# Operands of the MLP's first product 64 bytes further in memory, in tiles of 2176 bytes, beside a halved scratch for software DMA

## The chip, the cores and the metric

The kernel runs on one core of a Trainium2 chip. The metric is the device time of one execution in microseconds: 784.97 is the median of three runs of the kernel before (784.47 to 785.39). A difference of about 0.2% (1.57 us) is what a measurement of this kernel can tell from none.

## The reference

One layer of an encoder trunk over 512 rows of 1024 numbers: three token-mixing branches with gates, cross-attention into 256 memory tokens, and a squared-ReLU MLP, each sub-layer between two RMS norms. The change touches the last one:

```python
hf = rmsnorm(x, g_norm[l, 4])
yf = jnp.square(jax.nn.relu(hf @ w_up[l])) @ w_down[l]      # 1024 -> 4096 -> 1024
x = x + rmsnorm(yf, g_norm[l, 5])
```

## The kernel before

All products are float32 results made of three fast products. Every operand is split into a high part (a cast on ScalarE, line 152) and a low part (source minus high, on VectorE, line 153), and `mm3` (line 159) adds high by high, high by low and low by high in PSUM. So a weight block of 128 columns and an activation of 256 or 512 columns cost three matmuls, and each matmul has a weight load of its own (engine PEld in the profile, which runs beside PE). All of them are recorded at line 107, so groups of the profile are told apart by tile names.

Memory inside the core (224 KiB in each of 128 partitions, all tiles named by their bytes in one partition) is cut into pools. The pool of **slots** (line 79) has 27 tiles of 512 float32 numbers, 2048 bytes each. Nearly everything of that size passes through it: the parts of the first input `xg`, queries, merged branches `mg`, the residual `x`, scratch, and `xf`, the 8 pairs (high, low) of the normed input of the MLP (line 911), x by channel, channels in the partitions and the 512 rows along the tile. `by_channel` (line 725) writes `xf`. Weights and their parts stand in tiles of 4096 bytes in other pools (`parts_of`, line 117), whose names are `whi`/`wlo`, with a `u` behind for the MLP's first product and a `b` for its second.

The MLP works on quarters of its matrices, with seven block products instead of eight. In the first product (`two`, line 1109) one call makes two blocks of 128 of the 4096 inner channels: seven products of 12 matmuls each, 256 columns of x a time. Numbered as in the code, products 1, 5, 2 and 4 read `xf` (5 reads the second half of `xf0` to `xf3`, which a difference has been written over), products 6, 3 and 7 read the sums `xs6`, `xs3`, `xs7`. These three are made once (`quarters`, line 1040), in tiles of 4096 bytes that the code pushes 64 bytes on by an unused tile of 64 bytes ahead of them (`shift`, lines 1056 to 1066). Products 7 and 4 are held back into the middle of the second product's work. `steps` (line 1304) writes out the order by hand: 13 calls of `two` (steps "V") among 28 products of the second kind (`product`, line 1227, 512 columns of weights a time, activations as the stationary operand), one block made plainly ("U"), and the end (`down`, line 1252). Ahead of them stand five blocks made plainly over each half of the rows (216 matmuls into `ps` and 24 into `t`, 256 columns each, all reading `xf`). Loads and splits for a step are prepared two steps ahead of it.

Matmuls and transposes keep the program's order on TensorE; the other engines take theirs from a scheduler.

DMAs are issued by SyncE in hardware, and by GpSimd in software: 12 loads that add into a gate weight tile, 28 that add into an MLP weight tile, 8 loads of the memory tokens, 2 rows and 8 pieces of x (line 806). The program lets 8 software DMAs be under way: a ninth waits for the first. What GpSimd's DMAs are described by stands in a scratch at the start of the memory, 16384 bytes of each partition where nothing else is asked for.

Places in the built program (bytes in a partition): the weight parts start 64 past a multiple of 128 (832 past a multiple of 2048 all of them), the slots, and so `xf`, do the same, and so do the parts `mh` and `ml` of the memory tokens, which have the tile shape of `xs`. The `xs` tiles start at a multiple of 128 (896 past a multiple of 2048).

Of the kernel before, what the change touches and what calls it, by code (L numbers as in the profile page):

```python
# [10 lines left out]
F32 = mybir.dt.float32  # L11
F32R = mybir.dt.float32r
# [4 lines left out]
P = 128  # L17
D = 1024
S = 512
NT = S // P  # L20
KD = D // P
# [4 lines left out]
NSLOT, NHALF, NBIG = 27, 9, 8  # L26
# [33 lines left out]
def trunk(ctx: ExitStack, tc: tile.TileContext, wkvq, xT, xt0, memT, wst, cst, vec, rows, wsp, wpl, out):  # L60
    nc = tc.nc
# [6 lines left out]
    sl = ctx.enter_context(tc.tile_pool(name="sl", bufs=1))  # L68
# [7 lines left out]
    ones = tn.tile([P, 1], F32, name="ones")  # L76
    mhalf = tn.tile([P, 4], F32, name="mhalf")

    def slot(name, dt=F32, shape=None):
        return sl.tile(shape or [P, S], dt, name=name, tag="slot", bufs=NSLOT)  # L80

    late, extra = [], []

# [3 lines left out]
    def tiny(name, bufs=3):  # L87
        return tn.tile([P, 4], F32, name=name, tag=name, bufs=bufs)

    def pair(name, shape=None):  # L90
        return slot(name + "h", F32R, shape), slot(name + "l", F32R, shape)

    def pair_of(pool, name):
        return tuple(pool.tile([P, S], F32R, name=name + z, tag="act", bufs=2 * KD) for z in "hl")
# [39 lines left out]
    def wtile(i, fence=()):  # L134
        raw, hi, lo = wtiles(i)
        wdma[i] = nc.sync.dma_start(raw, wst[i]).ins
        with ExitStack() as c:
            for ins in fence:
                c.enter_context(tc.issue_after(ins))
            split(hi, lo, raw)  # L140
        return hi, lo
# [36 lines left out]
    def sqacc(sacc, src, first, n, eng=None, order=free):  # L178

        if first:  # L180
            order(nc.scalar.activation(sacc, src, AF.Square))
        else:
            sq = half("sq") if n == HALF else slot("sq")
            order(nc.scalar.activation(sq, src, AF.Square))
            order((eng or nc.vector).tensor_tensor(sacc, sacc, sq, op=ALU.add))

    class Rstd:
# [19 lines left out]
        def copied(self):  # L207
            n = self.t * P
            t = half("rb") if n == HALF else slot("rb")
            self.end = nc.vector.tensor_copy(t, self.spread()).ins  # L210
            return t


    with ExitStack() as c1:
        a = c1.enter_context(tc.tile_pool(name="a", bufs=1))
# [17 lines left out]

        x0 = [slot(f"x0_{k}") for k in range(KD)]
        xg = [pair(f"xg{k}") for k in range(KD)]
        sink = tn.tile([P, 8], F32, name="sink")

# [13 lines left out]
        for k in range(KD):  # L251
            split_scaled(*xg[k], x0[k], vc[:, V_G + k:V_G + k + 1], keep)
            for lo, hi in pieces if not k else [(0, NKVQ * P)]:
                r, h, l = (z[:, lo:hi] for z in raw[k])
# [32 lines left out]
        for b in range(4):  # L287
            q.append(pair(f"q{b}"))
            qend = split(*q[b], scaled(pq[b], f"qs{b}"))
# [342 lines left out]
        def merged(hf):  # L632

            if not mg:
                mg.extend(pair(f"mg{k}") for k in range(KD))
            for k in range(0, KD, 2):
                pt = bank()
                for kk2 in range(2):
                    for tb in range(2):
                        turn(pt[:, kk2 * HALF + tb * P:kk2 * HALF + (tb + 1) * P],  # L640
                             acc[2 * hf + tb, k // 4][:, (k % 4 + kk2) * P:(k % 4 + kk2 + 1) * P])
                for kk2 in range(2):
                    nc.scalar.copy(cut(mg[k + kk2], *halfcut(hf))[0], pt[:, kk2 * HALF:(kk2 + 1) * HALF])
                for kk2 in range(2):
                    hi, lo = cut(mg[k + kk2], *halfcut(hf))
                    end = nc.vector.tensor_tensor(lo, pt[:, kk2 * HALF:(kk2 + 1) * HALF], hi.bitcast(F32),
                                                  op=ALU.subtract).ins
            return end
# [93 lines left out]
    with ExitStack() as c2:  # L742
# [25 lines left out]
        def grow(name, at):  # L768
            g = big(name, F32, [P, 1024])
            nc.gpsimd.dma_start(g, rows[0:1, at:at + 1024].broadcast_to([P, 1024]))  # L770
            return g
# [136 lines left out]


        g3 = grow("g3", 3080)  # L910
        xf = [pair(f"xf{k}") for k in range(KD)]
        wom.update({i: wtile(T_OM + i, oend[0]) for i in (1, 3)})

        pso = {}
# [31 lines left out]
    with ExitStack() as c3:  # L946
        f = c3.enter_context(tc.tile_pool(name="f", bufs=1))
# [493 lines left out]
```

## Time and profile before

| | us |
|---|---|
| median of three runs | 784.97 |
| the profiled execution, whole time | 784.68 |
| its span, first to last instruction | 782.8 |
| PE busy | 773.3 |
| PEld busy | 671.0 |
| VectorE (DVE) busy | 611.5 |
| ScalarE (ACT) busy | 473.4 |
| GpSimd (POOL) busy | 66.6 |

How to read it: busy time is in us and as a share of the span. A matmul's duration holds its way through the array, so matmuls overlap in the records; how fast they follow each other is read from their starts in the timeline. A group's name is output<-moving operand,stationary operand, with the numbers of buffers left out where they end a name; PEld rows carry the name of the matmul that they load for. Granted clock is that of TensorE, 1.00 from the start to 772 us.

### The profile page before, as it was taken

How to read it: one execution, taken by the hardware profiler on the slowest of the kernel's cores; microseconds unless marked ns; L12 is line 12 of the kernel's file. 1: busy time of each engine (PE TensorE's matmuls, PEld its weight loads, DVE VectorE, ACT ScalarE, POOL GpSimd, SP SyncE). 2: the span in 40 equal slices, each digit the busy share in tenths (PEclk: the TensorE clock that was granted, in tenths of full speed). 3: DMA queues.
4: the chain of work that ended last, by engine and by line, in shares of the span. 5: the costliest groups of instructions: out<-in, count | busy, mean ns of one | idle time of the engine just before them, and what ended most of it. 6: DMA issues, size and time to landing. Idle time of an engine off the chain costs nothing.

```text
span 782.8 us, 11476 instructions
## 1 busy us (share of the span) xinstructions
PE 773.3 (99%) x4286; PEld 671.0 (86%) x4286; DVE 611.5 (78%) x931; ACT 473.4 (60%) x884; POOL 66.6 (9%) x93
## 2 busy tenths in 40 slices
PE   9999999999999999999999999999999999999996
PEld 8888878878888888788988899999988998899885
DVE  6488976898658657467759769899888998899866
ACT  7238779666562462444847585876666665567622
POOL 0000000201001000351100020001000100010001
PEclk9999999999999999999999999999999999999998
DMA  8325222745757132564331471776747764766612
GB/s 288 108 82 188 81 82 65 203 105 174 186 187 149 62 116 100 208 207 150 108 108 55 175 208 49 193 188 140 166 147 182 169 143 148 195 146 147 208 52 95
DMA packets 34423, 112.79 MB, mean 144 GB/s; under 512 B 4160, under 2 KB 4288, under 8 KB 34368
## 3 DMA queue, kind: packets, MB, share of 16 engines
q1 hardware_dynamic: 27152, 86.64, 32.8%
q0 software_dynamic: 7072, 25.17, 16.8%
q8 instruction: 33, 0.54, 0.3%
q10 hardware_dynamic: 144, 0.26, 0.1%
q14 instruction: 22, 0.18, 0.1%
HBM read 107.86 MB, written 4.19 MB: 143 GB/s over the span
## 4 chain that ended last, share of the span: by engine, by line
PE 90%; DVE 4%; ACT 4%; issue 1%; POOLq 0%; DVEq 0%; ACTq 0%
PE ps L107 51%; PE y L107 13%; PE v L107 10%; PE t L107 9%; PE z L107 6%; PE ps L110 2%; ACT s L335 2%; ACT s L345 1%; DVE s L327 1%; DVE wlo L153 1%; DVE mx L329 1%; ACT whi L152 1%; DVE yal L153 0%; ACT yah L152 0%; DVE t5l L153 0%
## 5 line engine op out<-in xcount | busy, mean ns | idle before, releaser
L153 DVE TENSOR_TENSOR wlo<-wraw,whi 128x1024 fp32r<-128x1024 f32 x58 | 71.5, 1240 | 40.8 <-ACT whi L152 40.6
L152 ACT CAST whi<-wraw 128x1024 fp32r<-128x1024 f32 x58 | 60.5, 1051 | 50.9 <-DMA wraw<-wst 24.6
L152 ACT CAST whiu<-wraw 128x512 fp32r<-128x512 f32 (+1 forms) x65 | 51.3, 792 | 47.3 <-DVE wraw L955 25.1
L153 DVE TENSOR_TENSOR wlou<-wraw,whiu 128x512 fp32r<-128x512 f32 (+1 forms) x65 | 57.4, 899 | 4.0 <-ACT whiu L152 3.1
L107 PE MATMUL y<-whib,whia 128*128 128x512 f32 x140 | 55.0, 393 | 0.0
L107 PE MATMUL y<-whib,wloa 128*128 128x512 f32 x140 | 54.7, 390 | 0.0
L107 PE MATMUL y<-wlob,whia 128*128 128x512 f32 x140 | 54.5, 389 | 0.0
L153 DVE TENSOR_TENSOR wlob<-q,whib 128x1024 fp32r<-128x1024 f32 x35 | 42.0, 1219 | 3.9 <-ACT whib L152 3.7
L153 DVE TENSOR_TENSOR wlog<-wq,whig 128x1024 fp32r<-128x1024 f32 x30 | 36.3, 1220 | 11.2 <-ACT whig L152 11.1
L152 ACT CAST whig<-wq 128x1024 fp32r<-128x1024 f32 x30 | 31.1, 1049 | 22.3 <-PE ps L107 11.2
L152 ACT CAST whib<-q 128x1024 fp32r<-128x1024 f32 x35 | 36.0, 1048 | 6.5 <-PE t L107 2.4
L107 PEld LDWEIGHTS y<-whib,wloa 128*128 128x128 f32 x140 | 26.3, 188 | 6.0
L1185 POOL DMA_DIRECT2D q<-wst x21 | 18.4, 876 | 149.0 <-DVE wlob L153 149.0
L107 PEld LDWEIGHTS y<-wlob,whia 128*128 128x128 f32 x140 | 26.3, 188 | 4.6
L107 PEld LDWEIGHTS y<-whib,whia 128*128 128x128 f32 x140 | 26.3, 188 | 4.5
L335 ACT ACTIVATE s<-s,ng 128x256 f32<-128x256 f32 x32 | 15.9, 501 | 11.2 <-DVE ng L331 11.2
L107 PE MATMUL z<-whib,whia 128*128 128x512 f32 x56 | 21.9, 392 | 0.0
L107 PE MATMUL z<-whib,wloa 128*128 128x512 f32 x56 | 21.8, 390 | 0.0
L107 PE MATMUL z<-wlob,whia 128*128 128x512 f32 x56 | 21.8, 389 | 0.0
L153 DVE TENSOR_TENSOR wlog<-wrawq,whig 128x1024 fp32r<-128x1024 f32 x12 | 14.7, 1224 | 8.4 <-ACT whig L152 8.4
L152 ACT CAST whia<-s 128x512 fp32r<-128x512 f32 x21 | 12.7, 619 | 12.8 <-PE t L107 11.9
L152 ACT CAST whig<-wrawq 128x1024 fp32r<-128x1024 f32 x12 | 12.6, 1051 | 11.9 <-issue 8.3
(1212 smaller groups left out, 2689.9 us busy)
## 6 DMA issues: line engine op xcount, KB each, us to landing
wraw<-wst SPq DMA_DIRECT2D x84, 512.0 KB, 3.3
q<-wst POOLq DMA_DIRECT2D x28, 512.0 KB, 6.6
q<-wst SPq DMA_DIRECT2D x14, 512.0 KB, 4.3
wrawq<-wst SPq DMA_DIRECT2D x12, 512.0 KB, 3.4
wq<-wst SPq DMA_DIRECT2D x12, 512.0 KB, 4.2
wq<-wst POOLq DMA_DIRECT2D x12, 512.0 KB, 6.3
xr<-xT SPq DMA_DIRECT2D x4, 512.0 KB, 6.4
x<-xt POOLq DMA_DIRECT2D x8, 256.0 KB, 7.9
```

Source lines behind the costliest of these rows:

```text
L107: keep(nc.tensor.matmul(*args, **kw))
L110: keep(nc.tensor.transpose(o, i, ident))
L152: return (order(nc.scalar.copy(hi, src)).ins, order(nc.vector.tensor_tensor(lo, src, hi.bitcast(F32), op=ALU.subtract)).ins)
L153: order(nc.vector.tensor_tensor(lo, src, hi.bitcast(F32), op=ALU.subtract)).ins)
L327: nc.vector.tensor_tensor(prob[i][:, 2 * bp:2 * bp + 2, :], raws[i][bp].rearrange("p (j k) -> p j k", j=2), mask, op=ALU.add)
L329: nc.vector.tensor_reduce(mx, prob[i], op=ALU.max, axis=AX.X)
L335: nc.scalar.activation(z, z, AF.Exp, bias=ng[:, b:b + 1], scale=0.125, accum_out=den[:, b:b + 1])
L345: nc.scalar.activation(z, z, AF.Identity, scale=rd[:, b:b + 1])
L1185: nc.gpsimd.dma_start(q, wst[i], accum_op=ALU.add)
```

## The change

Three things are changed, none of them an instruction:

- A slot is now 544 numbers (2176 bytes) and its user gets 512 of them from number `at` on, 0 everywhere but for `xf`.
- The 16 tiles of `xf` begin 16 numbers, that is 64 bytes, into their slot.
- The scratch for software DMA is 8192 bytes of a partition in place of 16384. The slots need 27 x 128 = 3456 bytes more than before, and 1152 were free at the end of the memory.

In the built programs every engine has the same instructions in the same order with the same waits, SyncE and GpSimd included. Only places differ: the small tiles and the weight parts move down by 8192, which leaves them 832 past a multiple of 2048; slots, counted from the first, move up by 128 bytes for each slot ahead of them, and all that follows the slots moves down by 4736. So everything still starts 64 past a multiple of 128, but `xf`, which now starts at a multiple of 128 as `xs` did and does. Counted in multiples of 256 or 512 bytes, slots and weight parts now lie 0, 128, 256 or 384 bytes apart instead of 0.

```diff
-    def slot(name, dt=F32, shape=None):
-        return sl.tile(shape or [P, S], dt, name=name, tag="slot", bufs=NSLOT)
+    def slot(name, dt=F32, shape=None, at=0):
+
+        t = sl.tile([P, S + 32], dt, name=name, tag="slot", bufs=NSLOT)[:, at:at + S]
+        return t if not shape or len(shape) == 2 else t.rearrange("p (a b) -> p a b", a=shape[1])
...
-    def pair(name, shape=None):
-        return slot(name + "h", F32R, shape), slot(name + "l", F32R, shape)
+    def pair(name, shape=None, at=0):
+        return slot(name + "h", F32R, shape, at), slot(name + "l", F32R, shape, at)
...
-        xf = [pair(f"xf{k}") for k in range(KD)]
+        xf = [pair(f"xf{k}", None, 16) for k in range(KD)]
...
-    nc = bacc.Bacc("TRN2", target_bir_lowering=False, num_devices=1)
+    nc = bacc.Bacc("TRN2", target_bir_lowering=False, num_devices=1, dynamic_dma_scratch_size=8192)
```

## The prediction

> **What bounds the kernel now.** The page first: which engine is busy, and which one the chain that ended last runs through.
>
> ```profile
> span 782.8 us, 11476 instructions
> PE 773.3 (99%) x4286; PEld 671.0 (86%) x4286; DVE 611.5 (78%) x931; ACT 473.4 (60%) x884; POOL 66.6 (9%) x93
> PE 90%; DVE 4%; ACT 4%; issue 1%; POOLq 0%; DVEq 0%; ACTq 0%
> ```
>
> TensorE is busy nearly all the time, and 90% of the chain lies on it. The change touches the MLP, so I read that stage by itself, in windows (length, then busy time of PE, PEld, DVE, ACT, POOL, the granted clock, the DMA share and GB/s): the blocks made plainly, the first steps, and the calls of `two` with the second product.
>
> ```profile
> 452.00:480.00 28.00, 28.00 (x235) 27.88 (x233) 21.82 (x46) 19.31 (x50) 4.51 (x7) 1.00 0.56 152
> 480.00:494.00 14.00, 14.00 (x76) 12.13 (x75) 13.79 (x26) 10.16 (x19) 0.86 (x1) 1.00 0.41 102
> 494.00:772.00 278.00, 278.00 (x1742) 251.62 (x1741) 243.15 (x344) 175.16 (x299) 23.32 (x28) 1.00 0.60 156
> ```
>
> PE never rests from 452 to 772 us, at full clock. But busy is not the same as peak: the matmuls' records overlap, so how far apart they start is what counts. The timeline of the first call of `two` (start, length) shows that:
>
> ```profile
> 494.02 0.28 PE L107 MATMUL t<-xf0h,whiu 128*128 128x256 f32 x1
> ...
> 498.34 0.28 PE L107 MATMUL t<-xs6h,whiu 128*128 128x256 f32 x1
> ...
> 501.17 0.40 PE L107 MATMUL y<-whib,whia 128*128 128x512 f32 x1
> ...
> 502.56 0.28 PE L107 MATMUL t<-xs7h,whiu 128*128 128x256 f32 x1
> ...
> 503.98 0.39 PE L107 MATMUL y<-whib,whia 128*128 128x512 f32 x1
> ```
>
> From 494.02 to 498.34 stand products 1, 5 and 2, 36 matmuls that read `xf`: 4.32 us, 120.0 ns each. From 498.34 to 501.17 stand products 6 and 3, 24 matmuls that read `xs6` and `xs3`: 2.83 us, 117.9 ns each. Product 7, 12 matmuls from `xs7` right behind a row of 512-column ones, takes 1.42 us, 118.3 each. Same columns, same weights pool, same banks of PSUM; only the moving tile is another. The records of single tiles (count, shortest/median/longest ns) say where the two nanoseconds sit:
>
> ```profile
> L107 PEld LDWEIGHTS t<-xf4l,whiu x20: 187/192/192, 496.9 to 729.7; 128*128 128x128 f32 x20
> L107 PE MATMUL t<-xf4l,whiu x20: 280/283/283, 497.0 to 729.8; 128*128 128x256 f32 x20
> L107 PEld LDWEIGHTS ps<-xf4l,whi x9: 192/192/192, 458.3 to 478.8; 128*128 128x128 f32 x9
> L107 PE MATMUL ps<-xf4l,whi x9: 283/283/283, 458.5 to 478.9; 128*128 128x256 f32 x9
> L107 PE MATMUL v<-xf4l,whiu x6: 280/283/283, 523.7 to 714.3; 128*128 128x256 f32 x6
> L107 PE MATMUL t<-xf4l,whi x2: 283/336/389, 481.8 to 488.8; 128*128 128x256 f32 x1, 128*128 128x512 f32 x1
> ...
> L107 PEld LDWEIGHTS t<-xs6l,whiu x28: 187/187/193, 498.3 to 721.0; 128*128 128x128 f32 x28
> L107 PE MATMUL t<-xs6l,whiu x28: 279/279/279, 498.5 to 721.1; 128*128 128x256 f32 x28
> ...
> L107 PEld LDWEIGHTS ps<-mh,wlo x32: 189/192/192, 368.3 to 379.5; 128*128 128x128 f32 x32
> L107 PE MATMUL ps<-mh,wlo x32: 281/283/283, 368.4 to 379.6; 128*128 128x256 f32 x32
> ```
>
> While `xf` streams, a weight load takes 192 ns and a matmul 283; while `xs6` streams, 187 and 279. The third pair decides between two readings. `xs6` differs from `xf` in the shape of its tile and in its place, 64 bytes off. `mh` has the tile shape of `xs6` and the place of `xf`, and it goes like `xf`: 192 and 283. So it is the place against the weights, not the shape.
>
> **The change, part by part.** *Number of matmuls.* The rows of `xf4l` count its readings of 256 columns: 20 + 9 + 6 + 1 = 36. A low part is read once in three matmuls, a high part twice, so a pair is read 108 times, and 8 pairs 864 times. In the code: 13 calls x 48, and 240 in the plain blocks.
>
> *Gain of each.* `xf` now lies against the weight parts as `xs` does. I take the mean of the three sums, (2.83 + 1.42) / 36 = 118.06 ns, so 1.94 ns less than 120.0. **864 x 1.94 = 1.68 us.** Were all like `xs6` and `xs3` it is 864 x 2.08 = 1.80, all like `xs7` 864 x 1.67 = 1.44. The first matmuls behind 512-column ones stand under 283 already (280 in the row of `v<-xf4l`), which takes off 0.1 at most. The 24 readings of 512 columns (one of 389 ns in the last row of `xf4l`) I cost at nothing: the load of some 190 ns lies under a stream as long as itself; at the same 1.94 they would give 0.05.
>
> *Does the time go through to the end?* Only if the weights are ready earlier too. VectorE writes the last part of each. Its timeline, where cover is thinnest:
>
> ```profile
> 491.87 0.68 DVE L955 TENSOR_TENSOR wraw<-wraw 128x512 f32<-128x512 f32 x1
> 492.47 0.68 DVE L153 TENSOR_TENSOR wlou<-wraw,whiu 128x512 fp32r<-128x512 f32 x1
> ...
> ACT whiu L152 <- PE v L107: 15.1, 7, 4.0
> ACT whia L152 <- PE t L107: 11.9, 3, 4.0
> ```
>
> The low part of product 5 is done at 493.15, and product 5 begins 12 matmuls after 494.02, at 495.46: 2.3 us ahead. What came before it, 240 matmuls, gains 0.47 us, so that margin holds, and the waits of 494 to 772 show the split engines waiting for TensorE (us, times, longest) in the steps behind, because they are ahead and lack a free buffer. If the cover were gone the loss would be what the stretch 480 to 494 can hold back, the 0.47 us, since VectorE is busy there for 13.79 of 14.
>
> *Slots 128 bytes further apart.* VectorE, ScalarE and DMAs find their operands at new places. Those off the path cost nothing as long as the margins stand. Matmuls that read a slot with 512 columns are another matter (they are the path): 950 of them, counted by tile (`xg` 648, `mg` 192, the parts for the end 84, `xf` 24). No row of before has a slot 128 or 256 bytes off the weights, so bounds: each might gain or lose what 64 bytes do, 1.94 ns, that is 1.84 us either way. I take nothing, since load and stream fit beside each other there:
>
> ```profile
> L107 PEld LDWEIGHTS ps<-wlo,mh x16: 187/188/192, 381.4 to 420.1; 128*128 128x128 f32 x16
> L107 PE MATMUL ps<-wlo,mh x16: 387/389/397, 381.7 to 420.3; 128*128 128x512 f32 x16
> ```
>
> At 512 columns the load is at 188, the short value, without any shift.
>
> *Scratch of 8 KiB.* No instruction is added. The most that GpSimd has under way is here:
>
> ```profile
> 341.21 0.56 POOL L770 DMA_DIRECT2D g<-rows  x1
> 341.77 3.78 POOL L806 DMA_DIRECT2D x<-xt  x7
> 348.29 0.55 POOL L806 DMA_DIRECT2D x<-xt  x1 [2.75 <-DMA g<-rows]
> 348.85 0.72 POOL L198 TENSOR_TENSOR rs<-ms,mhalf 128x2 f32<-128x2 f32 x1
> ...
> 360.50 0.61 PE L107 MATMUL ps<-cs,rs 128*128 128x128 f32 x4
> ...
> x<-xt POOLq DMA_DIRECT2D x8, 256.0 KB, 7.9
> ```
>
> Eight follow each other at 0.55 us, and only the ninth waits, as the program says. So 16 KiB hold eight at least, half of it four if room goes with size. With four, `rs` behind them would come some 8 us later, at 357, still ahead of the matmul at 360.50 that waits for it. I cost it at nothing. The Trainium skill ("DMA: Bandwidth & Descriptors", Terms) has a descriptor at 16 bytes, by which 8 KiB would be room for 512 of them on a ring, an estimate that no run here shows; by it, too, nothing waits.
>
> *Sum.* 784.68 - 1.7 = 783.0 for the profiled execution, whose span of 782.8 would be 781.1. The median stands 0.3 higher, which gives 783.3; I take 783.2.
>
> **The rivals.** *The place doesn't matter.* Then `xf` stays at 120.0 and the time at 785.0. This is what the Trainium skill's page "SBUF — State Buffer" has under "Who interferes with whom": TensorE has two independent read ports, one for the moving operand and one for weights, and never waits on anyone. By that rule the change is worth nothing; 192 against 187 ns speaks against it. Against the rival stands that `mh` and `xs6` differ in nothing but place and time. For it: `mh` was seen in another stage, and a cause in the steps of `two` themselves (which part of the weights, which bank) isn't excluded by it.
>
> *Finer steps of place count, to the good.* If lying 128 or 256 bytes off is as good as 64, three quarters of the 950 gain too, up to 1.4 us more: 781.8. The 188 ns above speaks against it.
>
> *Finer steps count, to the bad (slower).* If 128 bytes off collide harder than 0, the 950 lose. It turns the sum over from 1.7 / 950 = 1.8 ns each on; at the full 1.94 ns, and `xf` spoiled as well, since its tiles now lie 64, 192, 320 or 448 bytes off, it is 784.97 + 1.84 = 786.8. A weight load of over 213 ns would have to stick out there. The scratch could do it too, if it held no more than two DMAs: the nine above would come in pairs a landing (7.9) apart, `rs` at about 373, and TensorE would stand 13 us at 360.50. The count of four speaks against that.
>
> **How the numbers follow.** Forecast, 78%: the gain of 1.44 to 1.80 comes in, give or take the 0.4 us by which single runs stray. As 0.2% (1.57 us) is about what a measurement of this kernel tells from no change, and the forecast lies just over it, it splits into 53 faster and 25 the same. No effect, 9%: same. Finer steps to the good, 7%: faster. To the bad, with the scratch, 6%: slower. Together faster 0.60, same 0.34, slower 0.06. The range 782.0 to 785.0 holds the forecast with its stray and about half of "no effect"; it leaves out most of both finer cases.
>
> **What would show it.** `LDWEIGHTS` and `MATMUL` of `xf` at 187 and 279 to 280, in `ps` as in `t` and `v`: the mechanism. The step of products 1, 5 and 2 down from 4.32 to about 4.25 us. PE without a gap from 452 to 772, the stage shorter by 1.7: it goes through. The 512-column rows of `xg` and `mg` still at 389, else finer steps count. `xf` with some tiles at 283 and some at 279: the period is longer than 128 bytes. A wait of POOL in line 806 of more than 2.75 us: the scratch. It is wrong if the rows change and the end doesn't move, or the reverse.

## The result, and the profile after

The change made the kernel slower: 789.97 us as the median of six runs (789.39 to 790.47), against 784.99 of the kernel before beside it (784.32 to 785.39), a ratio of 1.0064 with a 95% interval of 1.0052 to 1.0075. It was forecast 1.8 us faster, and is 5 us slower.

The page of the changed kernel, the same three lines as before: span, busy time by engine, and the chain's shares.

```profile
span 788.3 us, 11476 instructions
PE 779.3 (99%) x4286; PEld 667.8 (85%) x4286; DVE 611.5 (78%) x931; ACT 473.7 (60%) x884; POOL 66.7 (8%) x93
PE 84%; DVE 4%; ACT 4%; issue 1%; POOLq 0%; DVEq 0%; ACTq 0%
```

The other engines are where they were (VectorE 611.5 in both, ScalarE 473.7 against 473.4). PE has 6.0 us more for the same 4286 matmuls, and its weight loads 3.2 us **less**. So its loads did not grow, and it hardly waited longer: the idle time in front of its matmuls is 2.4 us in all, against 2.2 before (own sum over the trace). Its matmuls start further apart. Where, one stage shows that was never in the forecast, the gates' products in front of the MLP. In the windows view (length, then busy time of PE, PEld, DVE, ACT and POOL with instructions, clock, DMA share, GB/s) the same 135 us of both kernels, first before, then after:

```profile
165.00:300.00 135.00, 135.00 (x597) 111.84 (x596) 95.14 (x103) 72.11 (x88) 6.98 (x8) 1.00 0.51 141
```

```profile
165.00:300.00 135.00, 135.00 (x582) 109.34 (x581) 94.59 (x102) 70.80 (x87) 6.99 (x8) 1.00 0.48 137
```

PE is busy all of it in both, at full clock, but gets through 582 matmuls instead of 597: 232 ns each against 226. The records of single tiles of the changed kernel (count, shortest/median/longest ns):

```profile
L109 PE MATMUL ps<-whig,x5h x24: 390/394/404, 166.6 to 271.9; 128*128 128x512 f32 x24
...
L109 PE MATMUL ps<-wlo,mh x16: 390/392/404, 388.2 to 427.4; 128*128 128x512 f32 x16
...
L109 PEld LDWEIGHTS t<-xf4l,whiu x20: 187/189/192, 504.0 to 735.1; 128*128 128x128 f32 x20
L109 PE MATMUL t<-xf4l,whiu x20: 277/279/283, 504.1 to 735.2; 128*128 128x256 f32 x20
...
L109 PE MATMUL t<-xs6l,whiu x28: 276/279/281, 505.6 to 726.6; 128*128 128x256 f32 x28
```

Before, the first of them stood at 389 throughout:

```profile
L107 PE MATMUL ps<-whig,x5h x24: 389/389/389, 164.8 to 267.4; 128*128 128x512 f32 x24
```

`wlo,mh` had 387/389/397; neither `x5h` (a gate's sum) nor `mh` is a slot, and both take longer. Starts say it more clearly than durations: the first 24 matmuls with `x5`, up to the next tile, first before, then after.

```profile
164.75 0.39 PE L107 MATMUL ps<-whig,x5h 128*128 128x512 f32 x1
...
170.19 0.39 PE L107 MATMUL ps<-whig,xg4h 128*128 128x512 f32 x1
```

```profile
166.60 0.40 PE L109 MATMUL ps<-whig,x5h 128*128 128x512 f32 x1
...
172.18 0.39 PE L109 MATMUL ps<-whig,xg4h 128*128 128x512 f32 x1
```

That is 5.44 us, 226.7 ns each, against 5.58 us and 232.5 ns.

In the rows of single tiles above, `xf4l` came down from a median of 283 to 279, as the forecast wanted. `xs6l` had 279 throughout and now has some at 276, though no line of the change names `xs`.

In the timeline of the changed kernel the three products that read `xf` begin at 501.20 and end where `xs6` begins:

```profile
501.20 0.28 PE L109 MATMUL t<-xf0h,whiu 128*128 128x256 f32 x1
...
505.44 0.28 PE L109 MATMUL t<-xs6h,whiu 128*128 128x256 f32 x1
...
508.18 0.39 PE L109 MATMUL y<-whib,whia 128*128 128x512 f32 x1
```

4.24 us for 36 matmuls, 117.8 ns each, where there were 4.32 and 120.0. And 2.74 us for the 24 behind them, 114.2 each, where there were 2.83 and 117.9.

Since durations say so little, I matched each matmul of the two traces and compared the distances to the next one's start, over the whole execution (an own calculation from the trace's starts):

| distance from one start to the next | matmuls | change, us |
|---|---|---|
| the first 29, up to 8 us from the start | 29 | +0.4 |
| 512 columns, back to back (under 280 ns in both) | 2363 | +9.6 |
| `xf`, 256 columns | 864 | -1.84 |
| `xs`, 256 columns | 468 | -0.95 |
| all others, waits and transposes among them | 561 | -1.1 |

The sum is +6.1 from the first matmul's start to the last one's; what follows the last one is shorter, and the span grew by 5.5. The first 29 stand by themselves because the two kernels begin differently: the changed one is done with the matmuls of `warm` 0.5 us earlier, and then waits for ScalarE where before does not:

```profile
7.35 0.50 PE L109 MATMUL ps<-xg0h,whik 128*128 128x512 f32 x1 [0.48 <-ACT whik L154]
```

The gain that was forecast is there, and a loss over five times as large (9.6 / 1.84) at the 512-column matmuls swallows it. By stages: from the first matmul that reads `xf` to the end of the calls of `two` (452.6 to 772.1 us before) the changed kernel needs 318.1 us in place of 319.5. Ahead of that stage it loses 7.5 us.

### The profile page after: what moved, and what is told of

It reads as the page before. It is cut to its first block, busy times and chain, and to the rows that moved or that the text cites. A ratio compares the mean times of both kernels' runs of the same rounds, so it can differ in the third digit from the quotient of the medians.

```text
span 788.3 us, 11476 instructions
## 1 busy us (share of the span) xinstructions
PE 779.3 (99%) x4286; PEld 667.8 (85%) x4286; DVE 611.5 (78%) x931; ACT 473.7 (60%) x884; POOL 66.7 (8%) x93
## 4 chain that ended last, share of the span: by engine, by line
PE 84%; DVE 4%; ACT 4%; issue 1%; POOLq 0%; DVEq 0%; ACTq 0%
PE ps L109 45%; PE y L109 13%; PE v L109 10%; PE t L109 9%; PE z L109 6%; PE ps L112 2%; ACT s L337 2%; ACT s L347 1%; DVE s L329 1%; DVE wlo L155 1%; DVE mx L331 1%; ACT whi L154 1%; DVE c L407 0%; DVE yal L155 0%; DVE c L413 0%
```

## The experiments

In the built program each tile's place is known, so every distance between two starts can be put beside the place of the next weights minus that of the operand that streams meanwhile, in bytes. The theory (A in the expectations): this difference sets the distance between starts, and 512-column matmuls pay where it is an odd multiple of 128. The change brings that about in two ways: slots 2176 bytes long lie at odd and even multiples by turns, and all that stands behind them moved down by 4736 = 37 x 128. Not all weight parts move by 8192: some stand behind the slots too and move by 4736 (324 of the 1092 reads of `whiu` and `wlou` in the built program are of such tiles). Rivals: the scratch; the offset of `xf` itself; the slots' own steps, and not their place against the weights; another period. All the kernels below keep the program's order.

**Parts of the change alone.** First the scratch on the kernel before.

```diff
-    nc = bacc.Bacc("TRN2", target_bir_lowering=False, num_devices=1)
+    nc = bacc.Bacc("TRN2", target_bir_lowering=False, num_devices=1, dynamic_dma_scratch_size=8192)
```

> The kernel before with nothing but the scratch of 8 KiB; every tile moves down by 8192 bytes, so no tile moves against another. Theory A (the place of the moving operand against the weights, counted in 512 bytes, sets how fast matmuls follow each other): 785.0, as before, 512-column matmuls 227 ns apart. Theory B (the halved scratch costs the 5 us): about 790. Theory C (the 64 bytes under xf cost them): 785.

784.32 us against 784.90, ratio 0.9992 (0.9982 to 1.0001). Halving the scratch costs nothing; theory B is out.

Then the changed kernel without the 64 bytes of `xf`.

```diff
-        xf = [pair(f"xf{k}", None, 16) for k in range(KD)]
+        xf = [pair(f"xf{k}") for k in range(KD)]
```

> The changed kernel with xf at the start of its slot. A: the loss stays and what xf gained goes: 790.7 to 792. B: about 790 to 792, no way to tell from A. C: back to 785.

790.16, ratio 1.0070 (1.0055 to 1.0085). The whole loss is still there, so the offset is not its cause, and C is out. But it is below the 790.7 that A wanted at the least: `xf` without its offset costs hardly more than with it. In its trace 592 readings of `xf` that are level with the next weights, modulo 256, start 118.1 ns apart, where level ones of before start 119.8 apart, and 270 that lie 128 off start 118.6 apart. Why level readings are faster between slots at unlike steps is open.

Then the changed kernel with an unused tile of 640 bytes behind the slots: the slots stay 2176 apart, and what follows them gets back to where it had been against the weights (4736 + 640 = 5376 = 21 x 256).

```diff
+    pb = ctx.enter_context(tc.tile_pool(name="pb", bufs=1))
+    pb.tile([P, 160], F32, name="behind")
```

> The changed kernel with 640 unused bytes behind the slots, so that everything behind them lies 0 past a multiple of 512 from the weight parts again, as before; slots and xf stay as in the change. A: the some 1060 matmuls of 512 columns with one operand in front of the slots and one behind them go from 232.5 back to 227 ns apart: 5.6 us less, xs loses 0.9: about 785.2, between 784 and 786.5. B and C: 790.

785.73, ratio 1.0010 (1.0001 to 1.0020). A tile that nobody reads takes 4.2 us off the changed kernel. What remains above before goes with the slots, the only tiles whose places against the others still differ from before.

The counter-trial, before with 128 unused bytes behind the slots and nothing else:

```diff
+    pb = ctx.enter_context(tc.tile_pool(name="pb", bufs=1))
+    pb.tile([P, 32], F32, name="behind")
```

> The kernel before with 128 unused bytes behind the slots and nothing else: slots keep their 2048 bytes, xf its place, the scratch its 16 KiB; only everything behind the slots moves by 128 against the weight parts. Theory A: this alone makes most of the loss: the some 1060 matmuls of 512 columns with one operand ahead of the pad and one behind go from 227 to 232.5 ns, 5.8 us more, xs gains up to 0.9: 789 to 790.8. Theory E (the slots' own 128-byte steps make it): 785 to 786.

789.60 against 785.35, ratio 1.0056 (1.0039 to 1.0073): most of the loss with the slots untouched. Its window of the gates is nearly as slow as the changed kernel's, 586 matmuls in 135 us:

```profile
165.00:300.00 135.00, 135.00 (x586) 110.09 (x585) 94.91 (x103) 71.75 (x88) 7.01 (x8) 1.00 0.49 141
```

That rules out the slots' own steps as the main cause; they wanted 785 to 786. The Trainium skill ("SBUF — State Buffer", "Who interferes with whom") has two independent read ports for TensorE, which never waits on anyone; 128 bytes of empty memory at 4.3 us speak against reading that as freedom from the place of its own operands.

**The period and the sides.** Here the slots of before are moved as a whole by 64, -64, 128 and 256 bytes against everything else: an unused tile ahead of them and one behind, 512 bytes together so that what follows them moves by a multiple of 256. For 64:

```diff
+    pa = ctx.enter_context(tc.tile_pool(name="pa", bufs=1))
+    pa.tile([P, 16], F32, name="ahead")
     sl = ctx.enter_context(tc.tile_pool(name="sl", bufs=1))
+    pb = ctx.enter_context(tc.tile_pool(name="pb", bufs=1))
+    pb.tile([P, 112], F32, name="behind")
```

> The kernel before with all 27 slots moved up together by 64 bytes (a pad of 64 ahead of them, one of 448 behind, so that nothing else moves in 512 bytes). Theory A: the place in 512 bytes counts for every matmul that has one operand in a slot. xf, 864 matmuls of 256 columns, from 120 to 118 ns: 1.7 us less. The 950 of 512 columns with a slot have no group of their own yet; the few rows at 64 to 448 in the trace of the change say 231, which is 3.3 us more: 786.5 in all. Had the 64 bytes been the lucky value for them too: 783.2. Theory D (only the spread of the places from slot to slot costs, one shift for all of them costs nothing): 783.2.

> The kernel before with all slots moved by 448 bytes, that is 64 below in 512 (pads of 448 and 64). A, with the sign of the 64: xf from 120 to 114 or 115.4, 4.0 to 5.2 us less; the 950 of 512 columns as with 64 above, unknown, 3.3 us more at 231 ns: 783 to 784.3. A without a sign: like the one 64 above. D: 780.

> The kernel before with all slots moved by 128 bytes (pads of 128 and 384). A: the 950 of 512 columns from 227 to 232.5, 5.2 us more; xf from 120 to 118.4, 1.4 less: 788.8. D: 785 or less. This is the offset that the change gave to everything behind the slots, here alone and the same for all slots.

> The kernel before with all slots moved by 256 bytes (pads of 256 and 256). A, with a period of 512: 512 columns from 227 to 230, 2.8 us more, xf to 118, 1.6 less: 786.2. A with a period of 256: 785.0, as before. D: 785.

| slots moved by | us | ratio (95%) |
|---|---|---|
| 64 | 787.23 | 1.0027 (1.0017 to 1.0038) |
| -64 | 784.69 | 0.9993 (0.9984 to 1.0002) |
| 128 | 788.71 | 1.0045 (1.0030 to 1.0060) |
| 256 | 785.02 | 1.0000 (0.9991 to 1.0010) |

At 128 it is what A gave (788.8). At 256 nothing changes: the period is 256 bytes, and 786.2, which a period of 512 would have given, is out. For 64 either way A came nearer than its rival, but was 0.7 us low for 64 and 0.4 low at the best for -64. Windows of the gates for 128 and, behind it, for 256:

```profile
165.00:300.00 135.00, 135.00 (x591) 110.85 (x590) 95.38 (x103) 72.30 (x89) 6.99 (x8) 1.00 0.51 141
```

```profile
165.00:300.00 135.00, 135.00 (x596) 111.40 (x595) 95.84 (x103) 72.08 (x88) 6.99 (x8) 1.00 0.51 142
```

From the starts of these four traces, of before, of the counter-trial and of the four trials below, in all of which the slots lie alike modulo 256, with the place of the next weights minus that of the moving operand counted modulo 256 (own calculation over distances under 280 and 160 ns, mean ns from start to start of each trace):

| next weights lie | 512 columns | 256 columns |
|---|---|---|
| level (0) | 227.0 to 228.1 | 119.6 to 119.8 (`xf`) |
| 64 above | 233.2 to 233.3 | 115.1 to 117.8 (`xs`), 117.0 to 117.8 (`xf`) |
| 128 off | 232.5 to 232.6 | 119.0 and 119.6 (`xf`) |
| 64 below | 229.1 to 229.6 | 117.4 to 118.0 |

The two columns run against each other. Level is best for 512 columns and worst for 256. These trials don't tell a matmul's own weights from the next ones: of the 1040 matmuls that are 128 off in the counter-trial 1013 have both there. The table accounts for the difference between 64 and -64: moving the slots up puts the 579 matmuls whose weights are a slot 64 above (+3.4 us), the 344 whose moving operand is one 64 below (+0.6), and `xf` too (-1.6): +2.4, and +2.3 was measured. Moving them down swaps the two counts: +1.0, +2.0, and `xf` at 117.0 for -2.4, +0.6 by this table, where -0.3 was measured.

**What is better than both.** `xs` of before put 64 bytes *below* the weights instead of above:

```diff
-                f.tile([P, 16], F32, name=f"shift{i}", tag=f"shift{i}", bufs=1)
+                f.tile([P, 112 if i == 0 else 16], F32, name=f"shift{i}", tag=f"shift{i}", bufs=1)
```

> The kernel before with the three xs sums 64 bytes below the weights' place in 512 bytes in place of 64 above (a pad of 448 bytes for one of 64); nothing else moves. A, with the sign of the 64 counting, as the trace of the change suggests (xs 113 to 115 ns apart where they lie 64 below): 468 matmuls x 2.5 to 4.5 ns less, 782.9 to 783.8. A without a sign: 785.0, 118 ns.

783.01, ratio 0.9976 (0.9967 to 0.9985), within what A gave. Matched with before, 1.2 us of it lie at `xs`, products 6 and 3 nearly alone (`xs3` 113.3 ns, `xs6` 114.9, `xs7` still 117.8), and 0.6 at the 512-column matmuls. In its records `xs6l` stands at 276:

```profile
L107 PE MATMUL t<-xs6l,whiu x28: 276/276/283, 498.8 to 719.6; 128*128 128x256 f32 x28
```

Then the change as it was meant: slots of 2304 bytes, so that slots and all behind them (27 x 256 bytes further) stay level with the weights, with `xf` 64 bytes on and the scratch halved.

```diff
-        t = sl.tile([P, S + 32], dt, name=name, tag="slot", bufs=NSLOT)[:, at:at + S]
+        t = sl.tile([P, S + 64], dt, name=name, tag="slot", bufs=NSLOT)[:, at:at + S]
```

> The change with slots of 2304 bytes in place of 2176, xf 64 bytes in as in the change, scratch of 8 KiB; all other tiles lie 0 or 256 past a multiple of 512 from each other. Theory A, now with a period of 256 (256 measured like 0): 512-column matmuls back to 227 ns, xf at 118: 785.0 - 864 x 1.9 ns = 783.3. If any distance between slots costs by itself: over 785.

782.85 against 784.96, ratio 0.9974 (0.9965 to 0.9983). The gates are back at 598 matmuls, and `xf` keeps its gain:

```profile
165.00:300.00 135.00, 135.00 (x598) 111.77 (x597) 96.46 (x104) 72.19 (x88) 6.99 (x8) 1.00 0.50 144
```

```profile
L109 PE MATMUL t<-xf4l,whiu x20: 279/279/284, 496.5 to 728.2; 128*128 128x256 f32 x20
```

Matched with before, its `xf` gives 1.65 us and its 512-column matmuls +0.2.

On that, `xf` 192 bytes into the slot (64 below the weights, level being taken modulo 256), and with it `xs` moved below as well:

```diff
-        xf = [pair(f"xf{k}", None, 16) for k in range(KD)]
+        xf = [pair(f"xf{k}", None, 48) for k in range(KD)]
```

> As the one with slots of 2304 bytes, with xf 192 bytes into its slot, that is 64 below the weights in 256. A with a sign: xf at 117 (as with all slots 64 below) to 115.4 ns (as xs there): 864 x 2.8 to 4.4 ns, 782.6 to 781.2. Without a sign: 783.3.

782.61, ratio 0.9971 (0.9960 to 0.9983): 0.2 less than with `xf` above, which the stray of single runs covers. `xf` stood at 117.5 to 117.8 ns and not near the 115 of `xs`, so the side is worth little to `xf`. By its time it stands at the very edge of what A gave with a sign, by its distances it is a miss.

```diff
-                f.tile([P, 16], F32, name=f"shift{i}", tag=f"shift{i}", bufs=1)
+                f.tile([P, 48 if i == 0 else 16], F32, name=f"shift{i}", tag=f"shift{i}", bufs=1)
```

> As the one before it, and the xs sums 64 below too (an unused tile of 192 bytes for the one of 64): 1.9 us less again, as measured for it alone: 780.7 to 779.3, the fastest of all. If the two gains overlap: no faster than 781.2.

781.47, ratio 0.9954 (0.9937 to 0.9971), the fastest of all: 3.5 us below before and 8.5 below the change. The 780.7 to 779.3 of two gains that add up were missed; it fits an overlap. It is 1.1 less than the one ahead of it, where `xs` alone had given 1.9. `xs` now stands like `xf`:

```profile
L109 PE MATMUL t<-xs6l,whiu x28: 281/281/281, 498.2 to 718.7; 128*128 128x256 f32 x28
```

Its starts are 117.8 ns apart, where they were 118.0 before and 115.3 with `xs` moved alone: the gain of `xs` is all but gone. What this run is faster by lies at the 512-column matmuls, whose mean went from 227.4 to 227.0 ns, 1.0 us over some 2300. Most of it, 0.85 us, lies at the first six matmuls behind 34 stretches of 256-column ones: by their place, first to sixth, their means lay between 225.3 and 237.3 ns, and now between 226.6 and 226.9 (own calculation). So the side of `xs` has an effect that depends on what else lies where; why is open.

## Why the prediction was wrong

**The step that failed** is "Slots 128 bytes further apart", in three of its parts.

- *Its count.* It priced "950" matmuls "that read a slot with 512 columns". But all that follows the slots moves by 4736 bytes, as the section on the change says, and 4736 is 37 x 128. The gates' sums, the outputs of the branches, the memory's parts and part of the MLP's second operands are not slots, stand behind them, and were left out. Matched against before, they make the larger half: 1001 matmuls with no slot in them are now 128 off the next weights, 227.1 to 232.6 ns, together +5.5 us. Matmuls with a slot come to +3.9: 360 of them 128 off (+1.8) and 572 at another difference (+2.2). (The four counts behind "950" add to 948, and the built program has 972; that changes nothing.)
- *Its price.* "Each might gain or lose what 64 bytes do, 1.94 ns" was a bound taken from 256-column rows. At 512 columns 128 bytes cost 5.2 ns, and 64 bytes 1.7 or 5.9 by the side.
- *Its reason for nothing.* "Load and stream fit beside each other there", read from loads of 188 ns. The load's duration doesn't show this collision at all. In the changed kernel the 32 matmuls `whi,yah`, none of them with a slot, went from 389 throughout to a median of 394 ns:

```profile
L107 PE MATMUL ps<-whi,yah x32: 389/389/389, 130.5 to 151.6; 128*128 128x512 f32 x32
```

```profile
L109 PE MATMUL ps<-whi,yah x32: 392/394/398, 131.7 to 153.4; 128*128 128x512 f32 x32
```

They have these loads there (the groups by line and shape: busy us and mean ns of one, then idle us before them):

```profile
L109 PEld LDWEIGHTS ps<-whi,yah 128*128 128x128 f32 x32 | 6.0, 188 | 1.5
```

Before, the same loads took as long:

```profile
L107 PEld LDWEIGHTS ps<-whi,yah 128*128 128x128 f32 x32 | 6.0, 188 | 1.3
```

The sign "a weight load of over 213 ns would have to stick out" was therefore no test of the rival.

**The rival "finer steps count, to the bad"** was the right mechanism, with 786.8 as its end and a chance of 6% shared with the scratch. It was short by the same count and the same price, so it ended 3.2 us below the 789.97 that came. It also took `xf` to be spoiled, which the runs don't bear out. The right price could not be read from before, where every slot is level with the weights; but an unknown price on 950, or rightly on some 1,900 matmuls of the path (1001 + 932), should have held far more than 6%.

**What was right.** *The number and gain of each:* forecast 864 x 1.94 = 1.68 us; measured 1.65 in the kernel with slots of 2304 bytes, and 1.84 in the changed one. That the changed kernel comes so near is partly luck: "`xf` now lies against the weight parts as `xs` does" holds there for 592 of 862 distances, modulo 256 (118.0 ns); the other 270 have the next weights on the other side and start 116.8 ns apart. The step of products 1, 5 and 2 was to be about 4.25 us and is 4.24. *The place and not the shape* of a tile sets it, as `mh` had said: `xf` itself, with its shape kept, gains when it is moved. *That it goes through to the end* held where nothing else lies differently: 782.85 with slots of 2304 bytes, against the forecast of 783.2. *The rivals "the place doesn't matter"* and *"finer steps, to the good"* are out. *The scratch at nothing:* the run with the scratch alone shows it, and the timeline of GpSimd in the changed kernel has a wait of 2.37 us, where over 2.75 was the sign against it:

```profile
353.40 0.55 POOL L808 DMA_DIRECT2D x<-xt  x1 [2.37 <-DMA g<-rows]
```

**What the signs said.** PE without a gap, and `xf` faster: both came, though not as narrowly as forecast (`xf4l` with loads at 187 to 192 and matmuls at 277 to 283, where 187 and 279 to 280 were wanted). The stage from 452 to 772 is 1.4 us shorter, where 1.7 was forecast, since its own 512-column matmuls lose 1.4, which the gains of `xf` (1.8) and `xs` (1.0) outweigh. So the stage that was priced came out nearly as forecast; the loss lies ahead of it, in products that were left out or taken at nothing. "`xf` with some tiles at 283 and some at 279: the period is longer than 128" came, and the period is 256. "512-column rows still at 389, else finer steps count" came the other way, 390 to 394; their medians of 392 and 394 are about 1% more, while the starts, 227.4 against 232.6, show 2.3%.

**A gain nobody forecast:** `xs` stands behind the slots, so moving it by an odd multiple of 128 put it 64 below the weights that stand ahead of the slots, instead of 64 above. That holds for 292 of its 468 distances (115.0 ns); for the other 176 the weights stand behind the slots and moved with it. That is the -0.95 us of the table.

**What stays open.** Why level and 64 off swap places between 256 and 512 columns. Why `xs` 64 below the weights gave 115.3 ns with `xf` level and 117.8 with `xf` beside it. Why only products 6 and 3 gained there and not 7. Which weights count, a matmul's own or the next. And why matmuls with a slot lose some 4 ns even where the next weights are level (548 of them at 230.8 ns in the changed kernel, 554 at 230.6 with the tile of 640 bytes behind): where their *own* weights lay 128 off they lost 5.9 ns in the changed kernel (118 matmuls), and level with both still 3.1 (430). Slots moved as a whole by 256 bytes show no such loss, so it goes with neighbours at unlike steps; no run took that apart. These 2 us of the loss have no shown cause.

## What to carry to other kernels

Where a tile's length is changed, everything that is allocated behind it moves as well: list the new places of all operands of the engine that bounds the kernel, not only of the tile that is meant. On this kernel, keep moving operands and weights of 512-column matmuls level modulo 256 bytes, and pad a slot by 256 rather than by 128. Judge TensorE's pace by distances between starts and not by durations, of matmuls or loads.

## What the runs showed of the hardware

- The place of the streamed operand against the weights (the next ones or its own, the trials don't tell), modulo 256 bytes, changes the pace of TensorE: 227.4 ns (level) to 233.3 ns at 512 columns, 115.1 to 119.8 ns at 256. 128 unused bytes between two pools cost 4.25 us of 785.35. Over the whole kernel the runs span 781.47 to 790.16 us with the same operations in the same order.
- The side counts: weights 64 bytes above the streamed operand cost 5.9 ns at 512 columns, 64 below 1.7. At 256 columns 64 above was the better side for `xs` in one trial (115.3 against 118.0) and no better in another (117.8).
- None of this shows in the duration of a weight load at 512 columns (188 ns in both), and little in that of a matmul (389 against medians of 392 to 394).
